# A hybrid encoder layer on one core: the gate's scale and bias moved into its drain, low parts in pieces, a search with one candidate

## The chip, the core and the metric

The kernel runs on one core of one Trainium2 chip. The metric is the device time of one execution in microseconds; the time of a kernel is the median of its runs. A core has five engines that run side by side, each with its own in-order queue: TensorE (PE in the rows; PEld is its weight load), VectorE (DVE), ScalarE (ACT), GpSimd (POOL) and SyncE (SP), which here issues most of the DMAs. Matmuls write PSUM, which TensorE, VectorE and ScalarE reach; GpSimd works on SBUF.

## What is computed

One layer of an encoder on 1024 frames of width 1024, in float32. Cut to what matters here:

```python
h = rmsnorm(x, g_pre_mix)
a_u, a_v, q, k, v, iq, ik, iw = split(h @ w_in)
# gate, over blocks of 128 frames, in 4 groups of 128 columns
vn = layernorm(a_v, sgu_ln_g, sgu_ln_b)
mixed = einsum('gij,bcjgd->bcigd', masked(sgu_w), vn) + sgu_b
out_a = a_u * mixed
# sparse attention: each frame keeps its 256 best earlier frames
score = sum_h iw * relu(iq_h @ ik.T)
idx = top_k(score, 256)
out_b = attention(q, k, v, idx, rel_bias)
x = x + rmsnorm(concat(out_a, out_b) @ w_o, g_post_mix)
x = x + rmsnorm(swiglu(rmsnorm(x, g_pre_ffn)), g_post_ffn)
```

## The kernel before, in words

**Matmuls in three.** Most projections multiply float32 numbers as a high part (the number rounded to fp32r) and a low part (what is left). `split_w` (lines 175 to 182) loads a weight tile, lets ScalarE write the high part and another engine, here always GpSimd, the low part in one subtraction over the whole tile, 1024 columns for most weights. `mm3` and `mm3x2` (lines 184 to 196) then issue high by high, high by low and low by high.

**Stages.** In order of the program: the indexer's query projection (`iqp`), its keys (`kp`), the gate's values (`wavp`, `evac_av`, lines 286 to 292, which also take mean and variance), the scores of the six upper row blocks (`sp`, lines 369 to 397), the gate projection u (`colgroup(evac_u)`, lines 403 to 412), the keys k (`colgroup(evac_k)`, 459), the values v (`rowgroup(wv, ...)`, 463), the queries q (`qgen`, 468), the search for each row's threshold (473 to 537), attention and output projection (an order written out by hand from line 951), and the feed-forward part, which fills the time from some 560 us to the end. `colgroup` (268 to 282) makes one block of 128 output columns for all 1024 frames: eight steps of six matmuls into one PSUM tile, then the drain, on VectorE in eight instructions of 128 columns. PSUM holds four tiles, handed out in rotation.

**The gate.** Lines 415 to 431 load the layer norm's scale and bias as rows broadcast to all partitions (`gb`), the mixing weights and their bias (`wb`), and mask the weights with a memset on VectorE. ScalarE then normalises each of the eight value tiles in place, and GpSimd multiplies it by the scale row and adds the bias row. `sgu_mix` (433 to 444) takes two tiles: eight 128-column matmuls into a PSUM tile (`mp`; the trace has two records for each), and on VectorE per tile one drain that adds the mixing bias, and one product with u. Four such mixes stand between the steps of the key projection (459 to 461).

**The search.** For each of the 128 rows of a score block, the 256th largest score is found bit by bit. `search` (487 to 533) does that for two groups of three blocks side by side, 31 rounds each: a candidate threshold, for each block a count of the scores above it, and a decision. The first group (blocks 6, 4, 3) counts on ScalarE with a sign and an accumulator, the second (7, 5, 2) on VectorE. The numbers between are 128 x 3, three columns for three blocks; per round each group has three such instructions on VectorE: the candidate from the bits found and a table of masks (`Kt`), the condition, and the new bits (`Bm`). The table is built from a small array that is loaded from memory (`bits`).

**What sets the order.** ScalarE and VectorE follow the program's order up to line 355; from there to line 951 a planner orders the instructions of every engine by its own model of their times; from 951 to 1065 ScalarE, VectorE, TensorE and GpSimd follow the written order, and after that the planner orders again. Each engine runs its queue strictly in the order that it was given.

Of the kernel before, what the change touches and what calls it, by code (L numbers as in the profile page):

```python
# [11 lines left out]
F32 = mybir.dt.float32  # L12
# [6 lines left out]
P = 128  # L19
# [9 lines left out]
TOPK = 256  # L29
EPS = 1e-6  # L30
NEG = -1.0e30
LOW = -3.0e38
QSCALE = float(np.float32(128 ** -0.5))
ISCALE = float(np.float32(np.float32(64 ** -0.5) * np.float32(8 ** -0.5)))


class Slots:
# [49 lines left out]

@with_exitstack
def tile_hybrid_block(ctx: ExitStack, tc: tile.TileContext, xT, x, wiq, wik, wct, wav, wv, gpre,
                      sguw, sgub, lng, lnb, relb, onehot, bits, wo, gpm, gpf, wg, wu, wd, gpo, out):  # L90
# [22 lines left out]
    def small(shape, name, dt=F32):  # L113
        return cpool.tile(shape, dt, name=name)
# [4 lines left out]
    def keep(n):  # L119
        keeps.append(n)  # L120
        return small([P, n], f"keep{len(keeps)}")
# [8 lines left out]
    def bcast_row(vec, n):  # L130
        return bass.AP(tensor=vec.tensor, offset=vec.offset, ap=[[0, P], [1, n]])
# [43 lines left out]
    def split_w(src, n, name, lo_engine):  # L175
        w = load(src, [P, n], "wf")
        hi = slot([P, n], name + "h", F32R)
        a.activation(hi, w, AF.Copy)
        lo = slot([P, n], name + "l", F32R)
        lo_engine.tensor_tensor(lo, w, hi.bitcast(F32), op=OP.subtract)  # L180
        free(w)
        return hi, lo

# [228 lines left out]
        pass  # L412


    gb = slot([P, 1024], "gb")
    dma.dma_start(gb[:, :512], bcast_row(lng, 512))
    dma.dma_start(gb[:, 512:], bcast_row(lnb, 512))
    wb = slot([P, 1024], "wb")
    dma.dma_start(wb[:, :512], sguw)
    dma.dma_start(wb[:, 512:], bcast_row(sgub, 512))  # L420
# [6 lines left out]
    for s in range(ST):  # L427
        av = KV[s][:, 512:]
        a.activation(av, av, AF.Identity, scale=rv[:, s:s + 1], bias=shift[:, s:s + 1])
        gp.tensor_tensor(av, av, gb[:, :512], op=OP.mult)  # L430
        gp.tensor_tensor(av, av, gb[:, 512:], op=OP.add)

    def sgu_mix(s):
        mp = ps([P, 2, 512], "mp")
        for d in range(2):
            av = KV[s + d][:, 512:]
            for g in range(4):
                pe.matmul(mp[:, d, g * P:(g + 1) * P], lhsT=av[:, g * P:(g + 1) * P],
                          rhs=wb[:, g * P:(g + 1) * P], start=True, stop=True)
# [22 lines left out]
    free(gb, wb)  # L462
    for i, _ in enumerate(rowgroup(wv, "wv", evac_v)):
        if i == 16:
            fetch()
# [4 lines left out]
        next(qgen)  # L470


    bt_c = small([P, 2, 31], "bt_c", I32)
    dma.dma_start(bt_c, bits)
    junks = st3[:, 512:].bitcast(I8)
    junk, junk_a = junks[:, :S], junks[:, S:]
    sign_c = small([P, 1], "sign_c", I32)
    v.tensor_scalar(sign_c, bt_c[:, 1, 0:1], 1, None, op0=OP.logical_shift_left)

    THR = {}  # L480

    def count(group, op, thr, cnt):
# [4 lines left out]
    def search(gi, group, on_act):  # L487
        g_ = len(group)
        cnt, neg = keep(g_), keep(g_)
        Bm, cond, cand, negi = (keep(g_).bitcast(I32) for _ in range(4))  # L490
        Kt = st5[:, 768 + gi * 128:768 + gi * 128 + 31 * g_].bitcast(I32).rearrange("p (a b) -> p a b", a=31)
        count(group, OP.is_ge, lambda i: 0.0, cnt)
        v.tensor_scalar(neg, cnt, float(TOPK), None, op0=OP.is_lt)
        v.tensor_scalar(negi, cnt, float(TOPK), None, op0=OP.is_lt)
        v.tensor_scalar(Bm, negi, 31, None, op0=OP.logical_shift_left)
        v.tensor_scalar(cand, Bm, 31, None, op0=OP.arith_shift_right)
        v.tensor_tensor(Kt, cand[:, None, :].to_broadcast([P, 31, g_]),
                        bt_c[:, 0, :, None].to_broadcast([P, 31, g_]), op=OP.bitwise_and)
        v.tensor_tensor(Kt, Kt, bt_c[:, 1, :, None].to_broadcast([P, 31, g_]), op=OP.bitwise_xor)
        if on_act:  # L500
            sgn, lim, negb = keep(g_), keep(g_), keep(g_).bitcast(I32)
            v.tensor_scalar(sgn, neg, -2.0, 1.0, op0=OP.mult, op1=OP.add)
            for i, b in enumerate(group):
                n = P * (b + 1)
                v.tensor_scalar(lim[:, i:i + 1], neg[:, i:i + 1], float(2 * n - 4 * TOPK + 1), float(2 * TOPK - n),
                                op0=OP.mult, op1=OP.add)
            v.tensor_copy(negb, Bm)
            v.tensor_copy(Bm, sign_c.to_broadcast([P, g_]))
        yield
        for k in range(31):  # L510
            v.tensor_tensor(cand, Bm, Kt[:, k, :], op=OP.bitwise_or)
            if on_act:
                for i, b in enumerate(group):
                    a.activation(junk_a[:, :P * (b + 1)], SC[b], AF.Sign, bias=cand.bitcast(F32)[:, i:i + 1],
                                 scale=sgn[:, i:i + 1], accum_out=cnt[:, i:i + 1])
                v.tensor_tensor(cond, cnt, lim, op=OP.is_ge)
            else:
                count(group, OP.is_ge, lambda i: cand.bitcast(F32)[:, i:i + 1], cnt)
                v.scalar_tensor_tensor(cond, cnt, float(TOPK), neg, op0=OP.is_ge, op1=OP.not_equal)
            v.scalar_tensor_tensor(Bm, cond, 30 - k, Bm, op0=OP.logical_shift_left, op1=OP.bitwise_or)  # L520
            yield
        if on_act:
            step = keep(g_).bitcast(I32)
            v.tensor_tensor(Bm, Bm, bt_c[:, 0, 0:1].to_broadcast([P, g_]), op=OP.bitwise_and)
            v.tensor_tensor(Bm, Bm, negb, op=OP.bitwise_or)
            v.tensor_copy(step, sgn)
            v.tensor_tensor(cand, Bm, step, op=OP.add)
            count(group, OP.is_ge, lambda i: cand.bitcast(F32)[:, i:i + 1], cnt)
            v.tensor_scalar(cond, cnt, float(TOPK), None, op0=OP.is_ge)
            v.copy_predicated(Bm, cond, cand)  # L530
        for i, b in enumerate(group):
            THR[b] = Bm.bitcast(F32)[:, i:i + 1]
        yield

    gens = [search(0, (6, 4, 3), True), search(1, (7, 5, 2), False)]
    while gens:
        gens = [g_ for g_ in gens if next(g_, 0) is None]

# [640 lines left out]
    return oh  # L1179


def _bits():
    bit = np.array([1 << i for i in range(30, -1, -1)], np.int64)
    t = np.stack([2 * bit - 1, bit]).astype(np.int32)
    return np.ascontiguousarray(np.broadcast_to(t[None], (P, 2, 31)))


def _layout(inp):
    x = inp["x"][0]
    w = inp["w_in"][0]  # L1190
    kp = lambda m: m.reshape(4, 2, P, 512).transpose(0, 2, 1, 3).reshape(4, P, 1024)
    ct = lambda m: m.reshape(KT, P, -1, P).transpose(2, 1, 0, 3).reshape(-1, P, 1024)
    vec = lambda m: m.reshape(KT, P).T
    return [
        ("xT", x.T.reshape(KT, P, S)),
        ("x", x),
        ("wiq", w[:, 2560:3072].reshape(KT, P, 512)),
        ("wik", w[:, 3072:3144].reshape(KT, P, 72).transpose(1, 0, 2).reshape(P, KT * 72)),
        ("wct", np.concatenate([ct(w[:, 0:512]), ct(w[:, 1536:2048]), ct(w[:, 1024:1536])])),
        ("wav", kp(w[:, 512:1024])),  # L1200
        ("wv", kp(w[:, 2048:2560])),
        ("gpre", vec(inp["g_pre_mix"][0])),
        ("sguw", inp["sgu_w"][0].transpose(2, 0, 1).reshape(P, 512)),
        ("sgub", inp["sgu_b"][0].reshape(512)),
        ("lng", inp["sgu_ln_g"][0]),
        ("lnb", inp["sgu_ln_b"][0]),
        ("relb", inp["rel_bias"]),
        ("onehot", _onehot()),
        ("bits", _bits()),
        ("wo", inp["w_o"][0].reshape(KT, P, D)),  # L1210
        ("gpm", inp["g_post_mix"][0]),
        ("gpf", inp["g_pre_ffn"][0]),
        ("wg", ct(inp["w_gate"][0])),
        ("wu", ct(inp["w_up"][0])),
        ("wd", inp["w_down"][0].reshape(FT, P, D)),
        ("gpo", inp["g_post_ffn"][0]),
    ]
# [20 lines left out]
```

## Time and profile before

| | us |
|---|---|
| median of 3 runs (1191.34 to 1196.72) | 1195.16 |
| the profiled execution | 1194.11 |
| its span, first to last instruction | 1191.9 |
| TensorE busy | 1138.1 |
| VectorE busy | 878.6 |
| ScalarE busy | 552.1 |
| GpSimd busy | 520.0 |

The mean granted clock of TensorE over the span is 0.983 of 2.4 GHz. In the rows further down a time is counted from the span's start. An operation is written with the tiles that it writes and reads (`cp` is a projection's PSUM tile, `mp` a mix's, `kv` and `qu` hold keys and gate values, queries and u; `keep` are the search's small columns, `sc` the scores, `wcl`, `wvl`, `wol` low parts, `lg` a softmax row). All operations have line 82, a helper that records them, so tiles tell them apart. The square bracket behind a timeline's row is the time for which the engine stood before it, and what released it.

### The profile page before, as it was taken

The numbers are of one execution on the slowest core, as the hardware profiler recorded it, in microseconds if no ns is written. First come the engines' busy times: TensorE is split into PE (matmuls) and PEld (weight loads), VectorE is DVE, ScalarE is ACT, GpSimd is POOL, SyncE is SP. The second block draws the span as 40 slices with busy tenths as digits, with TensorE's granted clock in tenths as the row PEclk, the third lists the DMA queues.
The fourth block names the chain that finished last, engine by engine and source line by source line (L and its number), as shares of the span: only waits on it lengthen the run. The fifth ranks groups of instructions, "written<-read, shape, count | busy, mean of one in ns | idle before, by whom it ended". The sixth has DMA issues, their size and how long they took to land.

```text
span 1191.9 us, 14894 instructions
## 1 busy us (share of the span) xinstructions
PE 1138.1 (95%) x5418; PEld 949.4 (80%) x5418; DVE 878.6 (74%) x1530; ACT 552.1 (46%) x987; POOL 520.0 (44%) x421
## 2 busy tenths in 40 slices
PE   7999999899999999977999999999999999999994
PEld 7778878788888888755778888888888888888883
DVE  4378999999786675687655868686868677776567
ACT  7465665657563445545454342424242424333431
POOL 5300148211132133685555555546473737463432
PEclk9999999899999999988999999999999999999997
DMA  9110411010140112312021212111212121211513
GB/s 365 71 45 1 142 54 57 18 51 18 46 133 18 37 36 71 131 46 71 1 71 36 71 36 71 49 65 64 65 42 71 36 71 38 70 54 55 175 53 142
DMA packets 24505, 81.82 MB, mean 69 GB/s; under 512 B 3024, under 2 KB 4080, under 8 KB 24432
## 3 DMA queue, kind: packets, MB, share of 16 engines
q1 hardware_dynamic: 24288, 80.87, 20.1%
q8 instruction: 43, 0.70, 0.2%
q14 instruction: 30, 0.25, 0.1%
q10 hardware_dynamic: 144, 0.00, 0.0%
HBM read 71.68 MB, written 9.18 MB: 68 GB/s over the span
## 4 chain that ended last, share of the span: by engine, by line
PE 76%; DVE 16%; ACT 4%; issue 2%; POOL 1%; DMA 1%; DVEq 0%; SPq 0%; POOLq 0%; ACTq 0%
PE gu L82 33%; PE dp L82 15%; PE cp L82 5%; PE y L82 5%; PE wavp L82 3%; PE iqp L82 3%; PE sp L82 3%; DVE keep L82 2%; PE wvp L82 2%; DVE sc L82 2%; PE L L82 2%; PE O L82 2%; DVE qu L82 2%; DVE columns L82 2%; ACT sc L82 1%
## 5 line engine op out<-in xcount | busy, mean ns | idle before, releaser
L82 PE MATMUL dp<-dop,fop 128*128 128x512 f32 x756 | 177.5, 389 | 0.1
L82 DVE TENSOR_TENSOR ac<-dp,ac 128x1024 f32<-128x1024 f32 (+1 forms) x130 | 150.1, 1181 | 25.3 <-PE dp L82 22.2
L82 PEld LDWEIGHTS dp<-dop,fop 128*128 128x128 f32 x756 | 141.8, 188 | 29.9 <-DVE ac L82 0.5
L82 ACT ACTIVATE guc<-gu 128x512 f32<-128x512 f32 x77 | 46.0, 598 | 216.8 <-PE gu L82 216.8
L82 DVE TENSOR_TENSOR wop<-wgu,wop 128x512 fp32r<-128x512 f32 x132 | 126.5, 980 | 26.4 <-ACT wop L82 25.1
L82 POOL TENSOR_TENSOR wgu<-wgu 128x512 f32<-128x512 f32 x66 | 100.9, 1528 | 70.0 <-DVE wop L82 47.5
L82 ACT ACTIVATE sc<-sc,keep,keep 128x896 int8<-128x896 f32 (+2 forms) x93 | 88.7, 954 | 63.1 <-DVE keep L82 61.6
L82 ACT ACTIVATE wop<-wgu 128x512 fp32r<-128x512 f32 x132 | 76.3, 624 | 86.6 <-POOL wgu L82 79.9
L82 DVE TENSOR_TENSOR guc<-gu,guc 128x512 f32<-128x512 f32 x66 | 45.6, 690 | 80.3 <-PE gu L82 73.6
L82 POOL TENSOR_TENSOR wcl<-wf,wch 128x1024 fp32r<-128x1024 f32 x12 | 28.8, 2400 | 155.3 <-DVE columns L82 65.7
L82 DVE TENSOR_SCALAR_CACHE_REDUCE sc<-sc,keep 128x1024 int8<-128x1024 f32 (+3 forms) x96 | 92.6, 965 | 2.2
L82 POOL TENSOR_SCALAR columns<-columns 128x1 f32<-128x1 f32 x84 | 31.0, 369 | 81.3 <-DVE columns L82 75.1
L82 PE MATMUL cp<-xh,wch 128*128 128x512 f32 x192 | 60.9, 399 | 4.3 <-DVE kv L82 4.3
L82 POOL TENSOR_TENSOR wx<-wgu 128x512 f32<-128x512 f32 x22 | 32.8, 1489 | 72.9 <-PE dp L82 62.2
L82 PE MATMUL gu<-b11h,wop 128*128 128x512 f32 x176 | 59.8, 401 | 4.8 <-DVE wop L82 3.3
L82 PE MATMUL gu<-b3h,wop 128*128 128x512 f32 x176 | 59.6, 400 | 4.8 <-ACT guc L82 2.6
L82 PE MATMUL cp<-xh,wcl 128*128 128x512 f32 x192 | 60.2, 395 | 1.3 <-POOL wcl L82 1.3
L82 PE MATMUL cp<-xl,wch 128*128 128x512 f32 x192 | 60.1, 394 | 0.0
L82 PE MATMUL gu<-b5h,wop 128*128 128x512 f32 x176 | 58.1, 391 | 1.5 <-DVE wop L82 0.8
L82 PE MATMUL gu<-b6h,wop 128*128 128x512 f32 x176 | 58.2, 392 | 1.1 <-ACT b6h L82 0.8
L82 PE MATMUL gu<-b7h,wop 128*128 128x512 f32 x176 | 58.0, 390 | 0.2 <-ACT guc L82 0.2
L82 PE MATMUL gu<-b21h,wop 128*128 128x512 f32 x176 | 58.1, 391 | 0.0
(237 smaller groups left out, 2935.8 us busy)
## 6 DMA issues: line engine op xcount, KB each, us to landing
wgu<-in_wg_dram SPq DMA_DIRECT2D x22, 512.0 KB, 3.4
wgu<-in_wu_dram SPq DMA_DIRECT2D x22, 512.0 KB, 4.1
wdr<-in_wd_dram SPq DMA_DIRECT2D x18, 512.0 KB, 3.5
wf<-in_wct_dram SPq DMA_DIRECT2D x12, 512.0 KB, 3.5
xt<-in_xT_dram SPq DMA_DIRECT2D x8, 512.0 KB, 6.5
xr<-in_x_dram SPq DMA_DIRECT2D x8, 512.0 KB, 9.5
wf<-in_wo_dram SPq DMA_DIRECT2D x8, 512.0 KB, 3.4
xres<-in_x_dram SPq DMA_DIRECT2D x8, 512.0 KB, 4.1
```

The source lines that it names most:

```text
L82: r = f(*args, **kw)
```

## The change

Three edits. The normalised gate values go into the mixing without scale and bias: the scale, one number per output partition of the mix, is loaded as a small column tile and multiplied in the drain, which becomes four instructions of 128 columns per tile; the bias row is mixed once by itself, and the result is added to the mixing bias. The low part of every split weight is written in pieces of 256 columns. The search keeps one candidate per row instead of bits and a table: a round flips the bit that failed and sets the next one.

```diff
     def split_w(src, n, name, lo_engine):
...
-        lo_engine.tensor_tensor(lo, w, hi.bitcast(F32), op=OP.subtract)
+        for c in range(0, n, 256):
+            m = min(n, c + 256)
+            lo_engine.tensor_tensor(lo[:, c:m], w[:, c:m], hi[:, c:m].bitcast(F32), op=OP.subtract)
...
-    gb = slot([P, 1024], "gb")
-    dma.dma_start(gb[:, :512], bcast_row(lng, 512))
-    dma.dma_start(gb[:, 512:], bcast_row(lnb, 512))
+    gain = small([P, 4], "gain")
+    dma.dma_start(gain, lng)
+    gb = slot([P, 512], "gb")
+    dma.dma_start(gb, bcast_row(lnb, 512))
...
         a.activation(av, av, AF.Identity, scale=rv[:, s:s + 1], bias=shift[:, s:s + 1])
-        gp.tensor_tensor(av, av, gb[:, :512], op=OP.mult)
-        gp.tensor_tensor(av, av, gb[:, 512:], op=OP.add)
+
+    def mix(o, av):
+        for g in range(4):
+            pe.matmul(o[:, g * P:(g + 1) * P], lhsT=av[:, g * P:(g + 1) * P], rhs=wb[:, g * P:(g + 1) * P],
+                      start=True, stop=True)
+
+    bp = ps([P, 512], "mp")
+    mix(bp, gb)
+    v.tensor_tensor(wb[:, 512:], bp, wb[:, 512:], op=OP.add)
+    free(bp, gb)
 
     def sgu_mix(s):
         mp = ps([P, 2, 512], "mp")
         for d in range(2):
-            av = KV[s + d][:, 512:]
-            for g in range(4):
-                pe.matmul(mp[:, d, g * P:(g + 1) * P], lhsT=av[:, g * P:(g + 1) * P],
-                          rhs=wb[:, g * P:(g + 1) * P], start=True, stop=True)
+            mix(mp[:, d], KV[s + d][:, 512:])
         for d in range(2):
             tmp, gate = QU[s + d][:, :512], QU[s + d][:, 512:]
-            v.tensor_tensor(tmp, mp[:, d, :], wb[:, 512:], op=OP.add)
+            for g in range(4):
+                c = slice(g * P, (g + 1) * P)
+                v.scalar_tensor_tensor(tmp[:, c], mp[:, d, c], gain[:, g:g + 1], wb[:, 512 + g * P:512 + (g + 1) * P],
+                                       op0=OP.mult, op1=OP.add)
             v.tensor_tensor(gate, tmp, gate, op=OP.mult)
...
         for k in range(31):
-            v.tensor_tensor(cand, Bm, Kt[:, k, :], op=OP.bitwise_or)
+            bit = 1 << (29 - k) if k < 30 else 0
             if on_act:
                 for i, b in enumerate(group):
                     a.activation(junk_a[:, :P * (b + 1)], SC[b], AF.Sign, bias=cand.bitcast(F32)[:, i:i + 1],
-                                 scale=sgn[:, i:i + 1], accum_out=cnt[:, i:i + 1])
-                v.tensor_tensor(cond, cnt, lim, op=OP.is_ge)
+                                 accum_out=cnt[:, i:i + 1])
+                v.tensor_scalar(nxt, cand, bit, None, op0=OP.bitwise_xor)
+                v.tensor_tensor(flip, cnt, lim, op=OP.is_lt)
+                v.scalar_tensor_tensor(cand, flip, 30 - k, nxt, op0=OP.logical_shift_left, op1=OP.bitwise_xor)
             else:
                 count(group, OP.is_ge, lambda i: cand.bitcast(F32)[:, i:i + 1], cnt)
-                v.scalar_tensor_tensor(cond, cnt, float(TOPK), neg, op0=OP.is_ge, op1=OP.not_equal)
-            v.scalar_tensor_tensor(Bm, cond, 30 - k, Bm, op0=OP.logical_shift_left, op1=OP.bitwise_or)
+                v.tensor_scalar(flip, cnt, float(TOPK), float(1 << (30 - k)), op0=OP.is_lt, op1=OP.mult)
+                v.scalar_tensor_tensor(cand, cand, bit, flip, op0=OP.bitwise_xor, op1=OP.bitwise_xor)
             yield
```

The load of `bits`, the table `Kt` and the steps that set them up go; the first candidate and, for ScalarE's group, a sign turned in its top bit and constant limits are set up instead, and the last step of that group is rewritten to match.

## Rows read from the trace of the kernel before

**Rows 1.** The page's busy table: engine, busy us (share of the span), instructions.

```profile
PE 1138.1 (95%) x5418; PEld 949.4 (80%) x5418; DVE 878.6 (74%) x1530; ACT 552.1 (46%) x987; POOL 520.0 (44%) x421
```

**Rows 2.** Table of stages: us, busy us of each engine, granted clock, DMA.

```profile
210.00:235.00 25.00, 20.70 (x96) 17.23 (x95) 24.17 (x73) 16.42 (x31) 5.58 (x3) 0.86 0.00 1
...
225.00:230.00 5.00, 5.00 (x12) 3.88 (x13) 4.93 (x15) 2.27 (x5) 0.00 (x0) 0.50 0.00 0
...
360.00:370.00 10.00, 9.66 (x60) 9.12 (x60) 8.96 (x15) 3.43 (x6) 5.44 (x2) 0.83 0.00 0
```

**Rows 3.** TensorE's timeline, 160 to 262: start us, us, operation, [idle before it <- releaser].

```profile
163.11 0.73 PE L82 MATMUL cp<-xh,wcl 128*128 128x512 f32 x2 [1.25 <-POOL wcl L82]
...
203.13 0.62 PE L82 MATMUL cp<-xh,wch 128*128 128x512 f32 x2
...
205.85 1.95 PE L82 MATMUL mp<-wb,kv 128*128 128x128 f32 x16
...
207.56 0.71 PE L82 MATMUL cp<-xh,wch 128*128 128x512 f32 x2
...
219.88 0.61 PE L82 MATMUL cp<-xh,wcl 128*128 128x512 f32 x2
...
224.79 1.19 PE L82 MATMUL cp<-xh,wch 128*128 128x512 f32 x2 [4.30 <-DVE kv L82]
...
230.05 2.32 PE L82 MATMUL mp<-wb,kv 128*128 128x128 f32 x16
...
259.59 0.47 PE L82 MATMUL wvp<-wvh,xh 128*128 128x512 f32 x1 [0.91 <-DVE kv L82]
```

**Rows 4.** VectorE's timeline, 160 to 230: the same columns.

```profile
160.37 0.16 DVE L82 TENSOR_TENSOR keep<-keep,sc 128x3 int32<-128x3 int32 x1
...
160.83 1.68 DVE L82 TENSOR_TENSOR qu<-cp,R 128x128 f32<-128x128 f32 x8 [0.30 <-PE cp L82]
...
163.62 2.32 DVE L82 TENSOR_TENSOR keep<-keep,keep 128x3 int32<-128x3 f32 x1
...
173.49 1.29 DVE L82 SCALAR_TENSOR_TENSOR keep<-keep,keep 128x3 int32<-128x3 int32 x2
...
178.45 0.27 DVE L82 MEMSET wb<- 64x256 f32 x1
...
196.97 1.28 DVE L82 TENSOR_TENSOR keep<-keep,sc 128x3 int32<-128x3 int32 x2
...
218.00 2.49 DVE L82 SCALAR_TENSOR_TENSOR keep<-keep,keep 128x3 int32<-128x3 f32 x2
...
222.98 1.67 DVE L82 TENSOR_TENSOR kv<-cp,R 128x128 f32<-128x128 f32 x8
...
225.09 1.28 DVE L82 TENSOR_TENSOR qu<-mp,wb 128x512 f32<-128x512 f32 x2
```

**Rows 5.** GpSimd's timeline in the same stretch.

```profile
160.68 2.37 POOL L82 TENSOR_TENSOR wcl<-wf,wch 128x1024 fp32r<-128x1024 f32 x1 [15.00 <-ACT wch L82]
...
173.40 13.79 POOL L82 TENSOR_TENSOR kv<-kv,gb 128x512 f32<-128x512 f32 x11
```

**Rows 6.** GpSimd's costliest groups by form: busy us, mean ns, idle before.

```profile
L82 POOL TENSOR_TENSOR wcl<-wf,wch 128x1024 fp32r<-128x1024 f32 x12 | 28.8, 2400 | 155.3 <-DVE columns L82 65.7 <-ACT wch L82 54.6 <-issue 35.0
...
L82 POOL TENSOR_TENSOR kv<-kv,gb 128x512 f32<-128x512 f32 x16 | 20.1, 1290 | 0.0
...
L82 POOL TENSOR_TENSOR b21l<-hraw,b21h 128x256 fp32r<-128x256 f32 x8 | 5.7, 731 | 0.0
```

**Rows 7.** Timelines of VectorE and TensorE, 325 to 362.

```profile
325.46 0.17 DVE L82 COPY_PREDICATED keep<-keep,keep 128x3 int32<-128x3 int32 x1
...
350.12 0.69 DVE L82 TENSOR_SCALAR lg<-lg,columns 128x896 f32<-128x896 f32 x1
...
357.65 2.55 DVE L82 TENSOR_SCALAR lg<-lg,columns 128x896 f32<-128x896 f32 x1
...
360.34 1.57 PE L82 MATMUL pp<-ident,lg 128*128 128x128 f32 x7 [2.31 <-DVE lg L82]
```

More of the change, by code (lines that the diff above doesn't have):

```diff
@@ L32 @@
 LOW = -3.0e38
+FIRST, SIGN = 1 << 30, -(1 << 31)
 QSCALE = float(np.float32(128 ** -0.5))
@@ L89, in tile_hybrid_block @@
 def tile_hybrid_block(ctx: ExitStack, tc: tile.TileContext, xT, x, wiq, wik, wct, wav, wv, gpre,
-                      sguw, sgub, lng, lnb, relb, onehot, bits, wo, gpm, gpf, wg, wu, wd, gpo, out):
+                      sguw, sgub, lng, lnb, relb, onehot, wo, gpm, gpf, wg, wu, wd, gpo, out):
     nc = tc.nc
@@ L461, in tile_hybrid_block @@
             sgu_mix(2 * (15, 20, 25, 30).index(i))
-    free(gb, wb)
+    free(wb)
     for i, _ in enumerate(rowgroup(wv, "wv", evac_v)):
@@ L470, in tile_hybrid_block @@
         next(qgen)
-    bt_c = small([P, 2, 31], "bt_c", I32)
-    dma.dma_start(bt_c, bits)
     junks = st3[:, 512:].bitcast(I8)
     junk, junk_a = junks[:, :S], junks[:, S:]
-    sign_c = small([P, 1], "sign_c", I32)
-    v.tensor_scalar(sign_c, bt_c[:, 1, 0:1], 1, None, op0=OP.logical_shift_left)
     THR = {}
@@ L485, in count, with search @@
                             accum_out=cnt[:, i:i + 1])
-    def search(gi, group, on_act):
+    def search(group, on_act):
         g_ = len(group)
-        cnt, neg = keep(g_), keep(g_)
-        Bm, cond, cand, negi = (keep(g_).bitcast(I32) for _ in range(4))
-        Kt = st5[:, 768 + gi * 128:768 + gi * 128 + 31 * g_].bitcast(I32).rearrange("p (a b) -> p a b", a=31)
+        cnt = keep(g_)
+        cand, ones, flip = (keep(g_).bitcast(I32) for _ in range(3))
         count(group, OP.is_ge, lambda i: 0.0, cnt)
[L493 to L499, printed above, removed]
+        v.tensor_scalar(flip, cnt, float(TOPK), None, op0=OP.is_lt)
+        v.tensor_scalar(ones, flip, 31, 31, op0=OP.logical_shift_left, op1=OP.arith_shift_right)
+        v.tensor_scalar(cand, ones, FIRST ^ SIGN if on_act else FIRST, None, op0=OP.bitwise_xor)
         if on_act:
-            sgn, lim, negb = keep(g_), keep(g_), keep(g_).bitcast(I32)
-            v.tensor_scalar(sgn, neg, -2.0, 1.0, op0=OP.mult, op1=OP.add)
+            lim, nxt = keep(g_), keep(g_).bitcast(I32)
             for i, b in enumerate(group):
[L504 to L508, printed above, removed]
+                v.memset(lim[:, i:i + 1], float(2 * TOPK - P * (b + 1)))
         yield
         for k in range(31):
-            v.tensor_tensor(cand, Bm, Kt[:, k, :], op=OP.bitwise_or)
+            bit = 1 << (29 - k) if k < 30 else 0
             if on_act:
@@ L514, in search @@
                     a.activation(junk_a[:, :P * (b + 1)], SC[b], AF.Sign, bias=cand.bitcast(F32)[:, i:i + 1],
-                                 scale=sgn[:, i:i + 1], accum_out=cnt[:, i:i + 1])
-                v.tensor_tensor(cond, cnt, lim, op=OP.is_ge)
+                                 accum_out=cnt[:, i:i + 1])
+                v.tensor_scalar(nxt, cand, bit, None, op0=OP.bitwise_xor)
+                v.tensor_tensor(flip, cnt, lim, op=OP.is_lt)
+                v.scalar_tensor_tensor(cand, flip, 30 - k, nxt, op0=OP.logical_shift_left, op1=OP.bitwise_xor)
             else:
                 count(group, OP.is_ge, lambda i: cand.bitcast(F32)[:, i:i + 1], cnt)
-                v.scalar_tensor_tensor(cond, cnt, float(TOPK), neg, op0=OP.is_ge, op1=OP.not_equal)
-            v.scalar_tensor_tensor(Bm, cond, 30 - k, Bm, op0=OP.logical_shift_left, op1=OP.bitwise_or)
+                v.tensor_scalar(flip, cnt, float(TOPK), float(1 << (30 - k)), op0=OP.is_lt, op1=OP.mult)
+                v.scalar_tensor_tensor(cand, cand, bit, flip, op0=OP.bitwise_xor, op1=OP.bitwise_xor)
             yield
         if on_act:
[L523 to L530, printed above, removed]
+            up, step = keep(g_).bitcast(I32), keep(g_).bitcast(I32)
+            v.tensor_scalar(cand, cand, SIGN, None, op0=OP.bitwise_xor)
+            v.tensor_scalar(step, ones, 2.0, 1.0, op0=OP.mult, op1=OP.add)
+            v.tensor_tensor(up, cand, step, op=OP.add)
+            count(group, OP.is_ge, lambda i: up.bitcast(F32)[:, i:i + 1], cnt)
+            v.tensor_scalar(flip, cnt, float(TOPK), None, op0=OP.is_ge)
+            v.copy_predicated(cand, flip, up)
         for i, b in enumerate(group):
-            THR[b] = Bm.bitcast(F32)[:, i:i + 1]
+            THR[b] = cand.bitcast(F32)[:, i:i + 1]
         yield
-    gens = [search(0, (6, 4, 3), True), search(1, (7, 5, 2), False)]
+    gens = [search((6, 4, 3), True), search((7, 5, 2), False)]
     while gens:
@@ L1179, in _onehot @@
     return oh
[L1182 to L1185, printed above, removed]
 def _layout(inp):
@@ L1204, in _layout @@
         ("sgub", inp["sgu_b"][0].reshape(512)),
-        ("lng", inp["sgu_ln_g"][0]),
+        ("lng", inp["sgu_ln_g"][0].reshape(4, P).T),
         ("lnb", inp["sgu_ln_b"][0]),
@@ L1208, in _layout @@
         ("onehot", _onehot()),
-        ("bits", _bits()),
         ("wo", inp["w_o"][0].reshape(KT, P, D)),
```

## The prediction

> **What bounds the kernel now.** The page's busy table comes first: TensorE is busy for 1138.1 of 1191.9 us [rows 1]. A change to VectorE, ScalarE or GpSimd work can therefore gain only what TensorE idles, or runs at the lower of its two clocks, in the stages that the change reaches. The table of stages shows the worst of these: from 210 to 235 us VectorE is busy for 24.2 of 25 us, and TensorE for 20.7, at a granted clock of 0.86 [rows 2].
>
> TensorE's own timeline names the holes [rows 3]. At 163.11 it had waited 1.25 us for a GpSimd low part; at 224.79 it had waited 4.30 us for VectorE to empty a PSUM buffer of the key projection; at 259.59 again 0.91 us. After the 4.30 us hole six pairs of 512-column matmuls take 5.26 us (224.79 to 230.05) where six took 2.72 (203.13 to 205.85), and the clock is granted at 0.50 from 225 to 230, which is 1.2 of 2.4 GHz [rows 2, 3]. There are four PSUM buffers in rotation; the block that started at 224.79 needed the one of the key block that TensorE had finished at 205.85, and VectorE set out to empty that at 222.98, 17.1 us late [rows 3, 4].
>
> Why is VectorE late? At 160.83 it was on time; it even waited 0.30 us for TensorE [rows 4]. Its timeline then shows three-column instructions, 0.16 us at 160.37, that take 2.32 us while a 2.37 us low part runs on GpSimd, and 1.29 for two while the gate's scale and bias run there, 11 instructions without a gap [rows 4, 5]. A reader sees the pattern by laying the two timelines side by side: each held instruction ends with the GpSimd instruction under it. From 163 to 220 us nine small instructions (the first in the row at 173.49, the last in that at 196.97) lose 9.6 us to the scale and bias, some 1.06 each, and six (the first at 163.62, the last in the row at 218.00) lose 10.8 us to low parts: 20.4 us, which covers the lag of 17.1 [rows 4].
>
> **The gate's scale and bias.** Removed: 16 GpSimd instructions, 20.1 us [rows 6]. They end on no chain of their own, but they hold VectorE for 9.6 us. Without them the lag at the second key block is at most 17.1 - 9.6 = 7.5 us, and TensorE gets to the block that needs the buffer some 14.4 us after it finished that one (219.88 + 0.45 - 205.85) [rows 3]. So the 4.30 us hole closes even if nothing else helps, and with it the low clock behind it: 5.26 - 2.72 = 2.5 us on the six pairs and 2.32 - 1.95 = 0.4 on the mix, 2.9 together [rows 3]. The 0.91 us hole has the same cause and goes too.
>
> Added: four gate matmuls on the bias row, ahead of the key projection. A mix of two tiles takes 1.71 us (205.85 to 207.56), so a half of that, 0.86 us, on TensorE's path [rows 3]. One more drain on VectorE, and the drain of the mix as four 128-column instructions per tile: eight of 128 columns take 1.67, so 0.84 us a tile against 0.64 (1.28 for two), 8 x 0.20 + 0.64 = 2.2 us on VectorE [rows 4]; it is hidden, since the lag shrinks by far more. That drain reads a scalar column as well, which these rows do not; I know no bound but nothing below it and, from a held small instruction, 1.1 us a tile above it, 9 us of lag in all, still about the spare.
>
> The bias matmuls also wait for the masking memset of the gate weights, which VectorE ran at 178.45 [rows 4]. A projection block takes 11 us on TensorE (207.56 to 220.3 less a mix), so the fourth gate block, two key blocks before 205.85, ended at 184, and would end at 182.5 without the 1.25 us [rows 3]. The memset is then done; cost 0, and up to 7 us if the planner puts the matmuls a block earlier. The loads: one of 16 bytes a row takes the place of a broadcast row, and the load of the search's bit table goes. They stand ahead of nothing that is waited for; cost 0, covered by the time until the memset.
>
> **The pieces.** A 1024-column low part takes 2.40 us, a 256-column one 0.73 [rows 6], so four take 2.9: GpSimd pays 0.5 us a part, hidden by the 20 us that it no longer has in this stage. The first piece of the late part would be done at 160.68 + 0.73 = 161.4, and TensorE came to it at 161.86 [rows 3, 5]: the 1.25 us goes. What VectorE gains lies between nothing (each small instruction of a cluster waits for its own piece) and three quarters of the 10.8 us; I take half, and TensorE's sum does not need it. In the attention the parts of the output weights meet a row scaling on TensorE's chain: 2.55 us against 0.69 for the same shape, and TensorE idles 2.31 us behind it [rows 7]; the clock is granted at 0.83 in the 10 us that follow, 1.7 us lost [rows 2]. With pieces the wait falls from 1.86 to some 0.6. I take 1.3 us and half of the clock's loss, 2.1 together; the ends are 0 (the scaling's neighbours wait at the next pieces) and 4.0 (the whole hole and the clock).
>
> That lower end is also what a rule would give. The rows show a held instruction ending with the one GpSimd instruction under it, and then the next held in its turn [rows 4, 5]. The Trainium skill (SBUF — State Buffer, Who interferes with whom) has it that the shared port pair is locked for a whole instruction by whichever came first. By that rule, and with every piece ahead of its VectorE neighbour, a part would hold VectorE as long as before, the 2.1 would be 0, and the sum 1185.6; the traces bear the lock out but not yet who comes first among pieces.
>
> **The search.** Per round one small instruction fewer in each of the two groups (on the ScalarE group's loop two in place of three, in the VectorE group two for three): 62 instructions, 0.16 us each [rows 4], 5 us where they run alongside others and up to twice that where each waits for the one before. The search ended at 325.46 [rows 7], and TensorE had projections to do all the way there, so 0 on its path. If that cover went, what the ten rounds between 161 and 224 save would count, some 3 us.
>
> **Sum**, against the profiled execution, 1194.11 us (span 1191.9 and 2.2 around it): - 4.3 - 2.9 - 0.9 - 1.25 + 0.86 - 2.1 = - 10.6, so 1183.5. The median shown is 1.05 us higher; I say **1184**. With the ends of the bounds the case gives 1180 to 1188.
>
> **Rivals.** (1) *The wait moves.* The planner makes a new order for all engines from its own clock, and a drain lands behind a search round elsewhere, so that some later block waits as long: 4.3 + 2.9 + 0.9 come back, 1192. For it: 62 instructions fewer and some 100 more reorder everything, and VectorE is busy for 97% of the time. Against it: 7 us of spare before the first buffer is missed. (2) *The pieces do nothing.* If TensorE waits for the last piece, 1.25 stays and grows by 0.5, and the attention's hole stays: 1183.5 + 1.75 + 2.1 = 1187.4. Against it: column ranges are followed elsewhere (a gate drain writes 128 columns of a tile at a time). (3) *Slower: the bias matmuls stand too early.* TensorE takes its queue in order. If they stand behind the second gate block (160.7) while the memset comes at 178.45, TensorE stands for 17.8 us, and pays 2.9 at the low clock behind it: 1183.5 + 20.7 = 1204. It decides from a wait of about 8 us on, at which the whole gain is used up. For it: the memset came 18 us after VectorE had last been on time, so the planner thinks its weights late. Against it: a planner that thinks them late puts the matmuls late too.
>
> **Chances.** A measurement of this kernel can tell about 0.5%, 6 us, from no change. Forecast 0.54, rival 2 0.12, rival 1 0.23, rival 3 0.11. The first two are faster by over 0.5% but for their upper ends, which touch the bound of 1189.2: 0.64. The same: 0.25, rival 1 and those ends. Slower: rival 3 from a wait of 14 us on, 0.11. The range reaches from 1177 (all bounds at their best, and the 4 us by which a run here lay under the median) to 1196 (rival 1 with that spread above it); it leaves out rival 3 and little else.
>
> **What would show it.** Right: TensorE without a hole over 1 us and at a granted clock of 1.00 from 161 to 260; GpSimd without the gate's 20.1 us, and its low parts as pieces of some 0.73 us; three-column VectorE instructions no longer than 0.9 us; the key blocks drained under 8 us after they end; the scaling after 357 us under 1.4 us. Wrong: a TensorE wait at the bias matmuls, a new wait for a PSUM buffer, a granted clock under 1 in that stretch, or the same 1194 with VectorE freed, which would mean that the holes were set by something other than VectorE's lag.

## The result, and the profile after

| | before | after |
|---|---|---|
| median | 1194.86 (4 runs) | 1181.40 (4 runs, 1178.18 to 1181.86) |
| the profiled execution | 1194.11 | 1181.17 |
| its span | 1191.9 | 1179.3 |
| mean granted clock | 0.983 | 0.985 |

The ratio is 0.9885 [0.9856, 0.9914]: 13.5 us faster, where 1184 was forecast from a profiled execution of 1194.11. All operations now have line 83.

The page's busy table, and the shares of the chain that ended last (which were TensorE 76% and VectorE 16% before):

```profile
PE 1135.1 (96%) x5426; PEld 947.9 (80%) x5426; DVE 848.8 (72%) x1513; ACT 544.3 (46%) x987; POOL 522.6 (44%) x511
...
PE 84%; DVE 9%; ACT 3%; issue 1%; POOL 1%; DMA 0%; DVEq 0%; SPq 0%; POOLq 0%; ACTq 0%
```

GpSimd is no less busy than in [rows 1], though 20.1 us of it are gone: its low parts take some 22 us more in pieces. A gain from its work can't be read from its total, only from when it ran.

The table of stages, for the stretches of [rows 2]:

```profile
210.00:235.00 25.00, 25.00 (x136) 21.61 (x135) 24.79 (x84) 12.38 (x26) 2.05 (x4) 1.00 0.07 22
...
350.00:360.00 10.00, 9.94 (x77) 9.42 (x78) 7.47 (x15) 4.73 (x7) 9.61 (x11) 1.00 0.11 29
360.00:370.00 10.00, 10.00 (x67) 8.90 (x66) 5.01 (x15) 2.97 (x5) 0.00 (x0) 1.00 0.06 25
```

TensorE is busy for the whole 25 us, at a granted clock of 1.00; before it was 20.70 us at 0.86. VectorE is as full as it was; it is only no longer late. TensorE's timeline, against [rows 3] and [rows 7]:

```profile
182.81 1.05 PE L83 MATMUL mp<-wb,gb 128*128 128x128 f32 x8
...
205.48 1.95 PE L83 MATMUL mp<-wb,kv 128*128 128x128 f32 x16
...
219.96 0.61 PE L83 MATMUL cp<-xh,wch 128*128 128x512 f32 x2
...
342.29 0.95 PE L83 MATMUL pp<-ident,lg 128*128 128x128 f32 x7 [1.44 <-DVE lg L83]
...
350.06 0.95 PE L83 MATMUL pp<-ident,lg 128*128 128x128 f32 x7 [0.71 <-DVE lg L83]
```

The reader is to see what is missing: the block at 219.96 has no bracket, where before it stood for 4.30 us. In the whole timeline no row from 160 us to 342 has one. The bias row is mixed at 182.81, without a wait. VectorE's timeline, against [rows 4]:

```profile
171.22 0.27 DVE L83 MEMSET wb<- 64x256 f32 x1
...
186.89 0.68 DVE L83 TENSOR_TENSOR wb<-mp,wb 128x512 f32<-128x512 f32 x1
...
206.99 1.67 DVE L83 TENSOR_TENSOR kv<-cp,R 128x128 f32<-128x128 f32 x8
...
209.72 2.15 DVE L83 SCALAR_TENSOR_TENSOR qu<-mp,gain,wb 128x128 f32<-128x128 f32 x8
...
295.53 0.17 DVE L83 COPY_PREDICATED keep<-keep,keep 128x3 int32<-128x3 int32 x1
...
348.98 0.93 DVE L83 TENSOR_SCALAR lg<-lg,columns 128x896 f32<-128x896 f32 x1
```

The second key block, which TensorE finished at 205.48, is drained at 206.99: a lag of 1.5 us in place of 17.1. The search's last step comes at 295.53; it was 325.46, 30 us later. The scaling at 348.98 takes 0.93 us, where the same one took 2.55.

The change ran once more, beside three of the experiments below (*e13_changed*): 1180.56 us (1178.22 to 1180.80, 4 runs) against 1195.43, ratio 0.9864 [0.9845, 0.9884]. TensorE has no hole between 160 us and 341 there either, but the lag at the second key block is 3.9 us: the 1.5 is of one execution and not of the kernel.

> The changed kernel itself, beside the one below on the same chip: 1181 us.

### The profile page after: what moved, and what is told of

Its sections match the earlier page's. It is cut to its first block, busy times and chain, and to the rows that moved or that the text cites. A ratio compares the mean times of both kernels' runs of the same rounds, so it can differ in the third digit from the quotient of the medians.

```text
span 1179.3 us, 14994 instructions
## 1 busy us (share of the span) xinstructions
PE 1135.1 (96%) x5426; PEld 947.9 (80%) x5426; DVE 848.8 (72%) x1513; ACT 544.3 (46%) x987; POOL 522.6 (44%) x511
## 4 chain that ended last, share of the span: by engine, by line
PE 84%; DVE 9%; ACT 3%; issue 1%; POOL 1%; DMA 0%; DVEq 0%; SPq 0%; POOLq 0%; ACTq 0%
PE gu L83 33%; PE dp L83 15%; PE cp L83 11%; PE y L83 5%; PE wvp L83 4%; PE wavp L83 3%; PE sp L83 3%; PE iqp L83 3%; PE L L83 2%; PE O L83 2%; DVE columns L83 2%; DVE sq L83 1%; PE pp L83 1%; PE kp L83 1%; DVE lg L83 1%
## 5 line engine op out<-in xcount | busy, mean ns | idle before, releaser
L83 POOL TENSOR_TENSOR wcl<-wf,wch 128x256 fp32r<-128x256 f32 x48 | 37.1, 809 | 161.5 <-DVE columns L83 65.4
L83 ACT ACTIVATE sc<-sc,keep 128x896 int8<-128x896 f32 (+2 forms) x93 | 80.2, 862 | 44.0 <-DVE keep L83 42.4
L83 ACT ACTIVATE lg<-lg,columns 128x1024 f32<-128x1024 f32 (+7 forms) x32 | 24.8, 775 | 86.9 <-DVE columns L83 86.9
```

The costliest lines, as they stand in the source:

```text
L83: r = f(*args, **kw)
```

## The experiments

Theory at the start: GpSimd's gate work made VectorE late, and taking it away gives most of the gain by itself; the pieces add the attention's part; the search adds nothing on TensorE's path. The rivals: a wait moves, or the search's edit is what counts. The first four runs are the edits one at a time, and the change without its pieces; before ran at 1195.23 (20 runs) beside them.

### The gate alone

*e1_gate*: the kernel before with the change's diff from `gb = slot` to the end of `sgu_mix`, and the two lines that follow from it (what is freed, and the layout of `lng`).

> The gate's edit alone (GpSimd's 16 instructions gone, bias mixed once, four drains a tile), low parts whole, old search. Theory of the lag: VectorE's 17.1 us at the second key block fall by the 9.6 us that the scale and bias held it for, under the 14.4 us at which TensorE misses the buffer, so the 4.3 and 0.9 us holes and the 2.9 us of low clock go, 0.9 is paid for the bias mix, and the 1.25 us hole and the attention's 2.31 us hole stay: 1187.5 us. Rival, every edit is needed (the lag must fall to nearly nothing): the 4.3 us hole stays at least in part, 1193 or more.

1196.79 us (1193.93 to 1198.34, 10 runs), ratio 1.0005 [0.9990, 1.0021]: no gain at all. Yet the projections went as forecast. TensorE finished the second key block at 204.13 and VectorE drained it at 211.66, a lag of 7.5 us, the very bound of the prediction (6.5 to 8.2 in the four runs with the gate's edit and whole low parts). TensorE has no hole between 195 and 320, and comes to the first attention scores at 310.61 in place of 320.91. Of these 10.3 us, 2.7 were there before the gate's work: the first gate block began at 136.16, against 138.87 before, and in every other run here it began within 0.8 us of that. The edit's own part is 7.6. Then TensorE stands. Its timeline, VectorE's, and the table of stages:

```profile
204.13 1.95 PE L82 MATMUL mp<-wb,kv 128*128 128x128 f32 x16
...
330.02 1.94 PE L82 MATMUL pp<-ident,lg 128*128 128x128 f32 x8 [8.85 <-DVE lg L82]
```

```profile
211.66 1.67 DVE L82 TENSOR_TENSOR kv<-cp,R 128x128 f32<-128x128 f32 x8
...
326.67 0.08 DVE L82 DVE_READ_ACCUMULATOR sc<-sc,keep 128x1 f32 x1
326.79 0.17 DVE L82 TENSOR_SCALAR keep<-keep 128x3 int32<-128x3 f32 x1
326.99 0.17 DVE L82 COPY_PREDICATED keep<-keep,keep 128x3 int32<-128x3 int32 x1
...
329.12 0.75 DVE L82 TENSOR_SCALAR lg<-lg,columns 128x1024 f32<-128x1024 f32 x1
```

```profile
321.00:332.00 11.00, 2.15 (x11) 2.02 (x11) 9.90 (x28) 2.59 (x5) 0.00 (x0) 0.62 0.31 97
```

The softmax row that TensorE wants is scaled at 329.12, on an engine that had the search's last rounds until 326.99. All that was gained went into an 8.85 us hole and the low clock behind it: eight records of 128 columns take 1.94 us at 330.02, where the bias mix's eight take 1.05. The search's end, for which TensorE did not wait before, was the next bound. It was so close already that the two timelines of the kernel before could have told:

```profile
330.44 0.76 DVE L82 TENSOR_SCALAR lg<-lg,columns 128x1024 f32<-128x1024 f32 x1
```

```profile
331.34 1.07 PE L82 MATMUL pp<-ident,lg 128*128 128x128 f32 x8
```

VectorE, which has no idle stretch from the search's last step at 325.46 [rows 7] to there, scaled the first softmax row until 331.20, and TensorE took it at 331.34. These 0.14 us are no more than the 0.15 between the two in the gate alone (329.87 to 330.02), where TensorE stood waiting, so there was next to nothing to spare. In the changed kernel the same row is scaled at 317.81 and taken at 322.37.

### The pieces alone

```diff
-        lo_engine.tensor_tensor(lo, w, hi.bitcast(F32), op=OP.subtract)
+        for c in range(0, n, 256):
+            m = min(n, c + 256)
+            lo_engine.tensor_tensor(lo[:, c:m], w[:, c:m], hi[:, c:m].bitcast(F32), op=OP.subtract)
```

> The 256-column pieces alone; GpSimd still scales and biases the gate values, old search. Theory of the lag: low parts held VectorE for 10.8 us between 163 and 220 before and for 4.3 in the changed kernel, so the lag falls from 17.1 to about 10.6, which is also under 14.4: the holes close without the gate's edit; 4.3, 2.9 and 0.9 go, so do the 1.25 and the attention's 2.31 with its low clock (3.3 in all): 1182.5 us, and the two edits do not add up. Rival, the holes belong to the gate's scale and bias: they stay, and only 1.25 and 3.3 go: 1190.

1192.58 us (1187.32 to 1193.76, 10 runs), ratio 0.9972 [0.9953, 0.9991], some 10 us above what was expected. TensorE's timeline:

```profile
222.94 1.19 PE L82 MATMUL cp<-xh,wch 128*128 128x512 f32 x2 [3.51 <-DVE kv L82]
...
332.01 1.94 PE L82 MATMUL pp<-ident,lg 128*128 128x128 f32 x8 [3.50 <-DVE lg L82]
...
361.14 0.96 PE L82 MATMUL pp<-ident,lg 128*128 128x128 f32 x7 [0.70 <-DVE lg L82]
```

The hole at the key projection stays (lag 16.3 us), and of the little gained before the attention, 3.0 us, all goes into a wait behind the search's end again. The attention's own hole shrinks to 0.70 as the pieces should make it. Nor do the pieces free VectorE in the projections: between 163 and 220 us low parts still hold VectorE's small instructions for 10.8 us, 9.2 of them in the gate's and keys' weights. VectorE's and GpSimd's timelines show why cutting them up bought so little there:

```profile
196.33 4.91 DVE L82 TENSOR_TENSOR keep<-keep,keep 128x3 int32<-128x3 f32 x1
```

```profile
197.01 4.21 POOL L82 TENSOR_TENSOR wcl<-wf,wch 128x256 fp32r<-128x256 f32 x6
```

One small VectorE instruction (0.16 us by itself) began under one of the gate's bias instructions and ended at 201.24, with the sixth of the pieces behind that, and not with the one under which it began.

### The search alone

*e3_search*: the kernel before with the change's search and without `bits`.

> The search with one candidate alone. Theory of the lag: the planner knows of the shorter rounds and puts more of them between two drains, so what is held stays what it was, some 20 us, and the lag some 17: all holes stay, 1194 us, with the search some 10 us earlier done. Rival, VectorE's load is what counts, and any of the three edits closes the holes: 1187.

1190.59 us (1188.89 to 1193.42, 5 runs), ratio 0.9948 [0.9931, 0.9965]. TensorE's timeline still has the hole at the key projection, longer than before and with a new one of 1.02 us ahead of it, and the hole in the attention; those of 1.25 and 0.91 us are gone:

```profile
214.15 2.02 PE L83 MATMUL mp<-wb,kv 128*128 128x128 f32 x16 [1.02 <-DVE kv L83]
...
225.64 1.19 PE L83 MATMUL cp<-xh,wch 128*128 128x512 f32 x2 [5.34 <-DVE kv L83]
...
359.80 0.95 PE L83 MATMUL pp<-ident,lg 128*128 128x128 f32 x7 [2.32 <-DVE lg L83]
```

The search now ends at 304.02, 21 us earlier. The execution that was profiled was the slowest of the five (1193.42), and its holes before 262 us sum to 6.4 us, as before (6.5), so where half a per cent of the median comes from stays open. The 20 runs of before lie 8.7 us apart, these five 4.5; with next to nothing to spare in the kernel before, an execution in which TensorE comes a little earlier would wait for the search, which would give that, but no trace here shows one.

### Gate and search, without the pieces

The edit is against the changed kernel:

```diff
-        for c in range(0, n, 256):
-            m = min(n, c + 256)
-            lo_engine.tensor_tensor(lo[:, c:m], w[:, c:m], hi[:, c:m].bitcast(F32), op=OP.subtract)
+        lo_engine.tensor_tensor(lo, w, hi.bitcast(F32), op=OP.subtract)
```

> The change without its pieces (gate and search). Theory of the lag: the key block's holes are closed as with the gate's edit alone, the low part's 1.25 us hole and the attention's hole (2.31 us and 1.7 of clock) are back: 1186.5 us. Rival, the search's relief carries the attention too (its search ends 30 us earlier in the changed kernel, and the first softmax rows start sooner): 1183 or less, with no hole behind the scaling.

1182.52 us (1180.67 to 1184.80, 4 runs), ratio 0.9888 [0.9865, 0.9910]. Against the median of before the gate alone is 1.6 us slower (its interval holds no change), the search alone 4.6 faster, and both together 12.7 faster. The gate's edit gains nothing without the shorter search, and the search alone a third of what both give: the gate lets TensorE come 9 us earlier, and the search is done by then (303.83). The gate with the pieces and the old search was not run. The expected return of the 1.25 us hole didn't come, since the planner's new order has the late low part early (at 159.00, where it was 160.68); with the pieces or the search alone it is gone as well, so it can't be credited to any one edit. The attention's holes are back, and with them the long scaling on VectorE:

```profile
342.01 0.96 PE L83 MATMUL pp<-ident,lg 128*128 128x128 f32 x7 [1.10 <-DVE lg L83]
351.39 1.36 PE L83 MATMUL pp<-ident,lg 128*128 128x128 f32 x7 [2.32 <-DVE lg L83]
```

```profile
348.70 2.54 DVE L83 TENSOR_SCALAR lg<-lg,columns 128x896 f32<-128x896 f32 x1
```

### The gate alone, with a shorter search

If the search's end was the bound of the gate alone, a search that stops sooner must give the gate its gain, with nothing else changed. This kernel leaves out the last three bits of each threshold.

```diff
-        for k in range(31):
+        for k in range(28):
```

> The gate's edit alone, and both searches stop after 28 of 31 rounds (the last three bits of the thresholds are left out). Gate alone: 1196.8, with the projections' holes closed but a new one of 8.85 us before the first transposed softmax row, and the search over at 326.7 us. Theory: that hole is the end of the search, which VectorE's queue has ahead of the first softmax row; three rounds of some 4 us less, the search is over near 314.5, the hole falls to about 0, and the time to 1187.5. Rival, the hole belongs to something else in the attention's start (the query projection's drains, the output weights' parts): it stays over 5 us, and the time over 1192.

1186.53 us (1185.19 to 1187.21, 4 runs), ratio 0.9933 [0.9910, 0.9955]; before ran at 1194.53 (9 runs) here. The search ends at 312.06, and the 8.85 us hole is gone: TensorE's first wait in the attention is the old one.

```profile
343.35 0.95 PE L82 MATMUL pp<-ident,lg 128*128 128x128 f32 x7 [1.11 <-DVE lg L82]
352.73 0.96 PE L82 MATMUL pp<-ident,lg 128*128 128x128 f32 x7 [2.32 <-DVE lg L82]
```

Three rounds of 31 were worth 10 us to the gate's edit, though TensorE waited for none of them in the kernel before.

### GpSimd's load given back

In the changed kernel GpSimd gets its 16 instructions back, but their results go to a tile that nobody reads, so that no one can wait for them.

```diff
         a.activation(av, av, AF.Identity, scale=rv[:, s:s + 1], bias=shift[:, s:s + 1])
+        gp.tensor_tensor(spare[:, :512], av, gb, op=OP.mult)
+        gp.tensor_tensor(spare[:, 512:], av, gb, op=OP.add)
```

> The changed kernel with 16 GpSimd instructions of 512 columns put back in the old place, on the same tiles but into a spare one that nobody reads. Theory of the lag: VectorE is held again while GpSimd runs, so the second key block is drained 11 to 16 us after it ends (1.5 in the changed kernel); the time stays at 1181 if that is under 14.4 and goes to 1189 if over. Rival, what the gate's edit gave came from the mixing no longer waiting for GpSimd's results: the drains stay within 5 us and the time at 1181.

1186.85 us (one run, against 1194.53): some 5 us of the change's gain are lost. The lag at the second key block is 16.9 us, and TensorE has a hole again:

```profile
223.61 1.13 PE L83 MATMUL cp<-xh,wch 128*128 128x512 f32 x2 [4.04 <-DVE keep L83]
```

So it is GpSimd's running alone that makes VectorE late. But it does so otherwise than thought, in a single row of VectorE's timeline. GpSimd's stands beside it:

```profile
191.92 10.59 DVE L83 TENSOR_TENSOR keep<-keep,keep 128x3 int32<-128x3 f32 x1
```

```profile
190.89 2.17 POOL L83 TENSOR_TENSOR wvl<-wf,wvh 128x256 fp32r<-128x256 f32 x3
192.98 8.82 POOL L83 TENSOR_TENSOR spare<-kv,gb 128x512 f32<-128x512 f32 x7
201.70 0.79 POOL L83 TENSOR_TENSOR wvl<-wf,wvh 128x256 fp32r<-128x256 f32 x1
```

Eleven GpSimd instructions run from 190.89 to 202.49 without a gap; the VectorE instruction of 0.16 us that began at 191.92, under the second, ends at 202.51, with the last of them.

### Which pieces matter

The change with pieces for the output projection's weights only:

```diff
-        for c in range(0, n, 256):
-            m = min(n, c + 256)
+        w_ = 256 if name == "wo" else n
+        for c in range(0, n, w_):
+            m = min(n, c + w_)
```

> Gate and search, with pieces for the output projection's weights alone. Theory: of the pieces only these matter once the lag is gone; the hole behind the scaling falls from 2.3 to 0.7 us and the low clock after it goes, 3 us less than gate and search alone (1182.5): 1179.5, no slower than the changed kernel at 1181.4. Rival, the other parts' pieces are needed to hold the lag down: a hole before 262 us, 1183 or more.

1180.89 us (1180.75 to 1181.50, 5 runs), ratio 0.9889 [0.9873, 0.9906]: as fast as the change, span 1179.1 against 1179.3. The lag at the second key block is 8.2 us in place of 1.5, and costs nothing. The medians alone don't tell the pieces' part: those of this run and of gate and search without pieces (1180.67 to 1184.80) overlap. TensorE's timeline does, with 0.71 us where that run had 2.32:

```profile
349.85 0.95 PE L83 MATMUL pp<-ident,lg 128*128 128x128 f32 x7 [0.71 <-DVE lg L83]
```

Of the pieces, those in the attention are all that TensorE feels.

### Why the search got so much shorter

The search was to end 5 to 10 us earlier; it ended 30 earlier. On ScalarE's group a round has as many small instructions as before, three, but one of them (`nxt`) is off the loop; on VectorE's it has two in place of three. So 31 instructions are gone, and not the 62 of the prediction. Two of the search's parts were put back into the change, one in each run: the sign's scale as a column of numbers, here ones, and one more dependent three-column step in each round of ScalarE's group.

```diff
+            v.memset(one, 1.0)
...
-                                 accum_out=cnt[:, i:i + 1])
+                                 scale=one[:, i:i + 1], accum_out=cnt[:, i:i + 1])
```

> The changed kernel with a column of ones given to ScalarE's sign as its scale, as the old search had a column of signs. In the old search one such count took 0.092 us longer than in the new (medians 0.921 and 0.829). Theory: that is the price of the scale column, 93 counts give 8.6 us, and the search is over at 303.5 us in place of 294.9; TensorE needs it only near 314, so the time stays at 1181. Rival, the price was of something else in the old round: 0.829 and 295 us as now.

```diff
+                v.tensor_scalar(cand, cand, 0, None, op0=OP.bitwise_xor)
```

> The changed kernel with one more three-column instruction at the end of each of the ScalarE group's rounds, behind the candidate (it changes nothing in it). Theory: each round of that group waits for it, 0.2 us, so the search is over some 6 us later, near 301, and the time stays at 1181. Rival, a small instruction finds room beside the other group's counts: no later than 297.

1181.09 and 1181.49 us (one run each, against 1195.43), under 1 us from the change beside them, so the cover holds for a search that ends at 310. The counts on ScalarE (after `x93:` the shortest, median and longest in ns, then when the first began and the last ended), for the change, with the scale column, and with the step:

```profile
L83 ACT ACTIVATE sc<-sc,keep x93: 705/829/1044, 129.3 to 288.0; 128x896 int8<-128x896 f32 x31, 128x640 int8<-128x640 f32 x31, 128x512 int8<-128x512 f32 x31
```

```profile
L83 ACT ACTIVATE sc<-sc,keep,keep x93: 796/921/1137, 129.4 to 304.0; 128x896 int8<-128x896 f32 x31, 128x640 int8<-128x640 f32 x31, 128x512 int8<-128x512 f32 x31
```

```profile
L83 ACT ACTIVATE sc<-sc,keep x93: 706/829/1047, 129.9 to 305.2; 128x896 int8<-128x896 f32 x31, 128x640 int8<-128x640 f32 x31, 128x512 int8<-128x512 f32 x31
```

Each undoes about half: 16.0 and 17.2 us on ScalarE's last count, 33.2 together, where 32.4 lie between 288.0 and the 320.4 of the kernel before. Each is also dearer than its own length: 93 counts x 0.092 us are 8.6 us, 31 steps x 0.16 are 5. That a round which misses its place beside the other group's counts waits for the next would explain it; no run shows that by itself.

### Two tries for more

In the changed kernel TensorE waits next at the entry of the feed-forward part, behind a chain of one-column steps on VectorE. Beside GpSimd's sums of 512 columns some of these take 1.15 and 1.21 us (at 501.53 and 511.01), where others of the chain take 0.17. *e7_entry_pieces* cuts those sums into columns of 256 in the first pass (and the four of `z` and `y` in halves); *e12_prep_early* also calls the first pass's preparation one step sooner.

```diff
+            for o, p, q, f in ((self.x, a11, a21, OP.subtract), (a21, a21, a22, OP.add),
+                               (a11, a21, a11, OP.subtract)):
+                for c in (slice(0, 256), slice(256, 512)) if self.p == 0 else (slice(0, 512),):
+                    gp.tensor_tensor(o[:, c], p[:, c], q[:, c], op=f)
```

> The changed kernel, and where the feed-forward part begins GpSimd's sums of 512 columns (the half sums of the normed rows and those of the first gate and up weights) in pieces of 256 as well. Theory: VectorE's one-column steps on the chain between 496 and 530 us are held for 0.46, 0.97, 0.98, 1.04, 0.47 and 0.99 us; with pieces each for 0.73 at most, so some 1.5 us less on the chain, 1180. Rival, GpSimd's own sums are the chain, and 0.15 us a piece for some 20 pieces make it 1 to 3 us longer: 1183.

> The kernel with the pieces at the feed-forward part's beginning (1179.2 us), and there the first split of the up weights is written ahead of the last block's normalisation steps instead of behind one of them. In that kernel TensorE waits 4.7 us for that split, whose low part VectorE makes only behind the steps of the chain. Theory: the wait falls to 2 us or less, the chain itself is 0.7 us later: 1177.5. Rival, the chain behind it is what bounds this stretch and TensorE waits as much a little later: 1179.5 or more.

1179.23 us (1178.42 to 1179.92, 5 runs), ratio 0.9874 [0.9857, 0.9890], and 1179.33 (1178.75 to 1181.13, 4 runs), ratio 0.9863 [0.9847, 0.9879]. Both are the fastest here by their medians, by 1.2 us against the change in the last call, which their ranges don't tell from it. The wait moves on TensorE's timeline, in the first to the weights that VectorE makes, in the second to `xres`, also VectorE's, so that for the second it is the rival that came: TensorE waits as much or more a little later. A row of each:

```profile
513.49 1.22 PE L83 MATMUL gu<-b11h,wop 128*128 128x512 f32 x2 [4.68 <-DVE wop L83]
```

```profile
520.29 1.94 PE L83 MATMUL tp<-ident,xres 128*128 128x128 f32 x8 [6.24 <-DVE xres L83]
```

## Why the prediction was right, and where it was not

TensorE's path, from one landmark to the next, in both profiled executions:

| first matmul of | before, us | after, us | difference | forecast |
|---|---|---|---|---|
| start to third gate block | 160.66 | 161.05 | +0.4 | 0 |
| to fourth gate block | 12.55 | 10.88 | -1.7 | -1.25 |
| to first key block (bias mix) | 10.88 | 11.69 | +0.8 | +0.86 |
| to fourth key block | 40.70 | 36.34 | -4.4 | -4.3 |
| to the values | 17.40 | 14.48 | -2.9 | -2.9 |
| to the queries | 44.72 | 43.52 | -1.2 | -0.9 |
| to the first output projection | 68.11 | 68.39 | +0.3 | 0 |
| to the second | 29.99 | 26.71 | -3.3 | -2.1 |
| to the end of the span | 806.85 | 806.20 | -0.6 | 0 |

The sum is -12.6 against -10.6.

- **The gate's hole and its low clock** were right to a tenth of a us, and so was the cause: with the load alone given back, a hole returned at 4.04 us, though by one long hold and not by many of 1.06. The bound of 7.5 us on the lag is what the gate alone showed.
- **The 1.25 us** came back, but not by the pieces: gate and search without them have it too, by the planner's new order. That term was right by luck.
- **The bias mix** came at 182.81 (forecast 182.5), with the memset done at 171.22. Rival 3 is excluded. The mix's drain takes 1.08 us a tile, not 0.84, and is hidden as argued.
- **The attention's term** was too small: with the hole at 0.71 the granted clock from 360 to 370 is 1.00, so all of the clock's loss came back and not half: 3.3 us, of which the hole is 1.6. The scaling is held for 0.2 us, not 0.6.
- **The pieces and the lock.** In the attention a held instruction got in between two pieces. By the Trainium skill (SBUF — State Buffer, Who interferes with whom) the pair is locked for one whole instruction by whichever came first, and the case in which every piece comes first would have given 1185.6; there it didn't happen. Elsewhere it did, for six pieces in a row (the pieces alone) and for ten instructions (the load given back). That is longer than one instruction, where the Trainium skill speaks of one, and the measurement decides. What VectorE gains from pieces was put at half of 10.8 us: alone it was nothing, in the change 6.5, since 4.3 us of holding are left (some 6.5 are left in the trace of *e13_changed*). It mattered to TensorE nowhere but in the attention.
- **The step that failed is the search: "0 on its path".** The prediction named its cover, TensorE's projections all the way to 325, and priced its loss at "some 3 us", from ten rounds between 161 and 224. But its own sum ended that cover: it moved TensorE 8.5 us forward without moving it in this step, and the cover had next to nothing to spare. The price of an uncovered search is the whole distance from TensorE's arrival to the row that is scaled behind the search's end, 8.85 us and the clock behind it in the gate alone.
- **The total came out right by luck.** The sum of -10.6 takes the gate and the pieces and nothing of the search. With the old search the gate alone and the pieces alone both wait at its end (8.85 and 3.50 us). The sum held because the search was in fact cut by 30 us, where the prediction had 5 to 10 from 62 instructions. Only 31 are gone. One step fewer on the loop of ScalarE's group was worth 17.2 us by itself, and a part as dear, 16.0, was not counted: the scale column on 93 ScalarE counts. The rows show 0.092 us for it; the Trainium skill (ScalarE: Activation LUTs, What ACT_TABLE_LOAD costs) gives some 93 ns for such a pointer operand, and the trace agrees.
- **A reading.** The low part under the instruction that took 2.32 us at 163.62 is not the one of 2.37 us in [rows 5], which had ended at 163.05, but the next, and with it the two ends agree (165.94 and 165.92):

```profile
163.53 2.39 POOL L82 TENSOR_TENSOR wcl<-wf,wch 128x1024 fp32r<-128x1024 f32 x1 [0.47 <-ACT wch L82]
```

- **Rival 2** (the pieces do nothing) is excluded in the attention. Ahead of it the pieces gave nothing that TensorE felt.
- **Rival 1** (the wait moves) didn't happen in the change. It is what happened in the gate alone and in the pieces alone, at the search's end and not at a drain.

## What to carry to other kernels

When a hole on the bounding engine closes, everything that used to be hidden by it is due that much earlier: move that engine forward by the whole sum, then ask of each cover named in the working whether it still ends in time. Edits tried one by one can read as nothing or little (here 0, 0.3 and 0.5 per cent) and be worth over one per cent together, so a null result for one calls for a look at which wait took its place. GpSimd work beside short VectorE instructions was paid for here by VectorE, and a long stretch of it without a gap once held a single short instruction for 10.59 us; whether gaps between the same instructions would have let it in was not run.

## What the runs showed of the hardware

- A three-column VectorE instruction that meets GpSimd doesn't always get in at the end of the one GpSimd instruction under it. It did so in the kernel before, 1.06 us at a time [rows 4, 5]; in two other runs it stood for 4.91 us (one bias instruction and six pieces) and 10.59 us (ten instructions). GpSimd ran without a gap in all three, so what decides between the two was not settled.
- Pieces of low parts take 0.73 to 0.76 us beside a busy VectorE too, as was taken from [rows 6], in 44 of the 48 below. The other four take 1.06 to 2.72 us, and make the mean 0.81. The longest (280.98 to 283.69) overlaps a VectorE scan of 1024 columns that ran until 283.16, so there it seems to be GpSimd that stood.

```profile
L83 POOL TENSOR_TENSOR wcl<-wf,wch 128x256 fp32r<-128x256 f32 x48 | 37.1, 809 | 161.5 <-DVE columns L83 65.4
```

- Holes of 1.44 and 0.71 us in the attention left the granted clock at 1.00 from 340 to 370 us, where 2.31 us (and the 1.10 before it) had it at 0.83 from 360 to 370.
- A drain of 128 columns from PSUM that also takes a scalar column costs 0.27 us (2.15 for eight), against 0.21 without one (1.67 for eight, also for the same instruction with a constant, the queries' drain).
